# Ordering TensorE's instructions in the mixers' loop of a streaming encoder step: the scheduler's order against the program's order

## The chip, the cores and the metric

The kernel runs on one core of one Trainium2 chip. The metric is the device time of one execution in microseconds (us). Of the kernel before there are three timed runs, whose median is 2215.13 us, and one profiled execution.

## The reference

One layer of a chunk-causal streaming encoder is computed for a prompt of 1024 frames and for a sample of 32 frames that comes with caches, at model width 1024. Three sub-layers follow one another:

```
h = adaln_in(x, ...);  x = x + 0.5 * g1 * rmsnorm(swiglu(h, w1_gate, w1_up, w1_down))
h = adaln_in(x, ...);  q, k, v of both mixers = split(h @ w_in)
oa, ob = mixers(...)
x = x + g2 * rmsnorm(concat([rmsnorm(oa), rmsnorm(ob)]) @ w_out)
h = adaln_in(x, ...);  x = x + 0.5 * g3 * rmsnorm(swiglu(h, w2_gate, w2_up, w2_down))
```

Mixer A is attention with 8 heads of 64, over a frame's own chunk of 64 and the 8 chunks before it. Mixer B has 8 query heads and 2 key and value heads over a window of 128, with a learned sink for each head. Both add a bias by relative distance. The shifts, scales and gates come from a matmul of SiLU(c) with `w_mod`. The newest rows of keys and values are outputs too. Everything is in float32.

## The kernel before, in words

Frames stand in three blocks `TB` of 384, 384 and 288 (the last holds 256 of the prompt and the 32 of the sample). The big products are written as three matmuls in a rounded float32 format: high times high, high times low, low times high (`mm3`, L325 to L327). The kernel goes through a first feed-forward part, the projections and mixers, the output projection, and a second feed-forward part.

The kernel is traced as a program, and a scheduler then puts each engine's instructions in an order of its own: `TileContext(nc, schedule_with_timeline_sim=True)` (L1352) takes, on a modelled clock, of the instructions whose inputs are there, the one that stands earliest in the program. `tc.manual_schedule(engines=...)` around a piece of the program makes the named engines keep the program's order there. The kernel uses that for SP, the engine that issues the transfers, during the start (L119 to L121, closed at L636).

The part around the change is the loop over the mixers' tiles, L1233 to L1269. There are 72 tiles, numbered by `n`. Tiles 0 to 35 are mixer B's: for each of four pairs of heads, one tile of the sample (`TileS`) and eight `TileB` of 128 frames each. Then come mixer A's: 36 to 44 for pair 0, 45 to 53 for pair 1, and from 54 on pairs 2 and 3 in turn, with their sample tiles at 54 and 55. A `TileA` has two halves, one for each head, and its row length L grows from 128 to 640 over the first five of its eight tiles.

A tile has three steps on TensorE, with a softmax between:

- `qk`: scores into PSUM (`S` L752, `Sb` L813 and L814, `Ss` L876 and L877, bank pool `p2` with 2 buffers); then bias add (DVE L754), maximum (DVE L758), exponential (ACT L761), reciprocal and scaling into `P` (L762 to L766).
- `tr`: transposes of `P` into `pp` (L776), `ppb` (L842) or `pps` (L902), in pool `p1` with 3 buffers, copied out to `PT`.
- `av`: `PT` times the values into `po` (L713), pool `pc` with 1 buffer, copied out to `O`. The two heads' matmuls alternate.

In the program, one turn of the loop holds, for each of its two halves: the scores of a tile ahead (two ahead for B, one ahead for A; `scores`, L1224), the transposes of this tile's half, in the first half also the `av` of the tile before, one step of a side task (`step(1)`), one step of the preparation of a coming pair of heads (`prep_step`), and then `fill(rate)`. `fill` puts in pieces of the projections that later tiles need (`pq` of `qk_proj`, `pv` of `v_proj`), so many that they last from turn 0 to 33 and from 37 to 53 (`STAGES`). `prepare` (L1007) loads the cached keys `ck`, writes out the new keys (`pkr`) and transposes the cached ones (`pkc` L1027). From turn 55 on the side tasks are `group_norm` (L1138): two squares on ACT (`sq` L364), sums on POOL (L368, L370), a sum over partitions on TensorE (`pss` L357), a reciprocal root on DVE, then, `WAIT` = 3 steps later, its broadcast on TensorE (`pr` L405), and the scaled values in a high and a low part (`o_hi`, `o_lo`, L1150 to L1155). From turn 67 to 71 each turn begins with one piece of the output projection (`out_piece` L1164, `wo`, 24 matmuls of `mm3`), which first demands that the group norms of its block are done.

Of the kernel before, what the change touches and what calls it, by code (L numbers as in the profile page):

```python
# [60 lines left out]
KB = 0  # L61
SPLIT = "vav"
LEAD_B = 2
MANUAL = False
WAIT = 3
PREP = 3
STAGES = ((0, 34), (37, 54))
# [7 lines left out]
def encoder_step(ctx: ExitStack, tc, x_prompt, x_sample, cache_a_k, cache_a_v, cache_b_k, cache_b_v,  # L75
# [1156 lines left out]

    with tc.manual_schedule(engines={mybir.EngineType.PE}) if MANUAL else ExitStack():  # L1233
        waits[0] = WAIT
# [121 lines left out]
```

## Time and profile before

| what | before |
|---|---|
| median of 3 timed runs | 2215.13 us (2212.06 to 2218.25) |
| the profiled execution's own time | 2217.6 us |
| its span in the profile | 2215.8 us |
| mean granted TensorE clock over the span | 0.984 |
| TensorE busy, share of the span | 98% |
| DVE, ACT, POOL busy, share of the span | 56%, 31%, 8% |
| the mixers' loop in the trace | from 916.6 us to 1329 us |

The rows of the profile name a source line, an engine, an operation and `out<-in` by the names in the program. PE is TensorE. A matmul's busy time is the modelled length of one instruction, and matmuls overlap, so what a matmul takes of TensorE in a run of its like is read from the distance between two starts. `PEclk` is the share of full clock that TensorE was granted. A float32 matmul stands as two records.

### The profile page before, as it was taken

How to read it: one execution, taken by the hardware profiler on the slowest of the kernel's cores; microseconds unless marked ns; L12 is line 12 of the kernel's file. 1: busy time of each engine (PE TensorE's matmuls, PEld its weight loads, DVE VectorE, ACT ScalarE, POOL GpSimd, SP SyncE). 2: the span in 40 equal slices, each digit the busy share in tenths (PEclk: the TensorE clock that was granted, in tenths of full speed). 3: DMA queues.
4: the chain of work that ended last, by engine and by line, in shares of the span. 5: the costliest groups of instructions: out<-in, count | busy, mean ns of one | idle time of the engine just before them, and what ended most of it. 6: DMA issues, size and time to landing. Idle time of an engine off the chain costs nothing.

```text
span 2215.8 us, 33976 instructions
## 1 busy us (share of the span) xinstructions
PE 2161.6 (98%) x14012; PEld 2068.6 (93%) x14012; DVE 1239.1 (56%) x2425; ACT 697.8 (31%) x1450; POOL 179.2 (8%) x281
## 2 busy tenths in 40 slices
PE   6999999999999999899999899999999999999998
PEld 4999999999999999799787589999999999999998
DVE  5788667874333497677444865785333333333336
ACT  4411111111121253576444663542111111111133
POOL 1100000000000023001110313220000000000000
PEclk8999999999999999899999899999999999999999
DMA  9253334434122352111112121424211111111122
GB/s 323 93 153 118 111 96 124 143 101 129 39 66 69 101 184 93 38 39 30 50 30 62 46 77 67 134 86 120 66 58 39 57 39 39 58 38 58 39 69 79
DMA packets 200623, 186.03 MB, mean 84 GB/s; under 512 B 7597, under 2 KB 169813, under 8 KB 199317
## 3 DMA queue, kind: packets, MB, share of 16 engines
q1 hardware_dynamic: 200468, 183.87, 27.1%
q8 instruction: 110, 1.80, 0.3%
q14 instruction: 45, 0.36, 0.1%
HBM read 164.12 MB, written 22.86 MB: 84 GB/s over the span
## 4 chain that ended last, share of the span: by engine, by line
PE 90%; DVE 4%; DMA 3%; ACT 1%; issue 1%; POOL 0%; SPq 0%; ACTq 0%; DVEq 0%; POOLq 0%
PE dn L325 7%; PE dn L326 7%; PE dn L327 7%; PE gate L327 7%; PE gate L326 7%; PE up L327 7%; PE up L326 7%; PE gate L325 7%; PE up L325 7%; PE po L713 3%; PE S L752 2%; PE pq L325 2%; PE pq L327 2%; PE pq L326 2%; DMA raw<-in_w_gate_dram 1%; PE pp L776 1%
## 5 line engine op out<-in xcount | busy, mean ns | idle before, releaser
L326 PE MATMUL gate<-h_lo,w 128*128 128x384 f32 (+1 forms) x1056 | 340.2, 322 | 4.0 <-DVE h_lo L446 4.0
L325 PE MATMUL dn<-gg,w 128*128 128x384 f32 (+1 forms) x1056 | 341.4, 325 | 1.1 <-DVE facc L581 1.0
L581 DVE TENSOR_TENSOR facc<-dn,facc 128x768 f32<-128x768 f32 (+1 forms) x240 | 212.9, 889 | 230.2 <-PE dn L327 229.9
L326 PE MATMUL dn<-gg,w 128*128 128x384 f32 (+1 forms) x1056 | 340.6, 323 | 0.6 <-DVE gg L554 0.6
L325 PE MATMUL gate<-h_hi,w 128*128 128x384 f32 (+1 forms) x1056 | 341.0, 323 | 0.0
L327 PE MATMUL gate<-h_hi,w 128*128 128x384 f32 (+1 forms) x1056 | 340.4, 322 | 0.0
L325 PE MATMUL up<-h_hi,w 128*128 128x384 f32 (+1 forms) x1056 | 340.2, 322 | 0.0
L326 PE MATMUL up<-h_lo,w 128*128 128x384 f32 (+1 forms) x1056 | 340.0, 322 | 0.0
L327 PE MATMUL dn<-gg,w 128*128 128x384 f32 (+1 forms) x1056 | 340.0, 322 | 0.0
L327 PE MATMUL up<-h_hi,w 128*128 128x384 f32 (+1 forms) x1056 | 339.9, 322 | 0.0
L304 DVE TENSOR_TENSOR w<-raw,w 128x1024 fp32r<-128x1024 f32 x187 | 231.5, 1246 | 150.5 <-ACT w L303 150.3
L303 ACT ACTIVATE w<-raw 128x1024 fp32r<-128x1024 f32 x187 | 195.7, 1056 | 266.1 <-PE dn L327 103.5
L550 ACT ACTIVATE sl<-gate 128x384 f32<-128x384 f32 (+1 forms) x132 | 60.9, 462 | 563.9 <-PE gate L327 560.9
L551 DVE TENSOR_TENSOR sl<-sl,up 128x384 f32<-128x384 f32 (+1 forms) x132 | 68.5, 519 | 292.1 <-PE up L327 286.1
L326 PEld LDWEIGHTS gate<-h_lo,w 128*128 128x128 f32 x1056 | 198.6, 188 | 4.6 <-DVE h_lo L446 4.6
L325 PEld LDWEIGHTS dn<-gg,w 128*128 128x128 f32 x1056 | 199.2, 189 | 1.6 <-DVE facc L581 1.2
L326 PEld LDWEIGHTS dn<-gg,w 128*128 128x128 f32 x1056 | 199.2, 189 | 1.0 <-DVE gg L554 0.9
L327 PEld LDWEIGHTS dn<-gg,w 128*128 128x128 f32 x1056 | 199.1, 189 | 0.0
L325 PEld LDWEIGHTS gate<-h_hi,w 128*128 128x128 f32 x1056 | 198.7, 188 | 0.1
L327 PEld LDWEIGHTS gate<-h_hi,w 128*128 128x128 f32 x1056 | 198.7, 188 | 0.0
L327 PEld LDWEIGHTS up<-h_hi,w 128*128 128x128 f32 x1056 | 198.7, 188 | 0.0
L325 PEld LDWEIGHTS up<-h_hi,w 128*128 128x128 f32 x1056 | 198.5, 188 | 0.0
(224 smaller groups left out, 3367.4 us busy)
## 6 DMA issues: line engine op xcount, KB each, us to landing
raw<-in_w_mod_dram SPq DMA_DIRECT2D x56, 512.0 KB, 4.0
raw<-in_w_gate_dram SPq DMA_DIRECT2D x54, 512.0 KB, 4.0
raw<-in_w_up_dram SPq DMA_DIRECT2D x54, 512.0 KB, 4.7
raw<-in_w_down_dram SPq DMA_DIRECT2D x54, 512.0 KB, 4.5
raw<-in_w_in_dram SPq DMA_DIRECT2D x18, 512.0 KB, 4.3
wm<-in_w_mod_dram SPq DMA_DIRECT2D x8, 1024.0 KB, 7.4
raw<-in_w_out_dram SPq DMA_DIRECT2D x13, 512.0 KB, 4.5
xr<-xs SPq DMA_DIRECT2D x16, 384.0 KB, 3.5
```

The lines of the kernel that those rows point to most:

```text
L303: ae.activation(w[:, 0], r, AF.Copy)
L304: ve.tensor_sub(w[:, 1], r, w[:, 0])
L325: te.matmul(ps, w[:, 0, k], hi, start=start, stop=False)
L326: te.matmul(ps, w[:, 0, k], lo, start=False, stop=False)
L327: te.matmul(ps, w[:, 1, k], hi, start=False, stop=stop)
L550: ae.activation(sl[:, :w], ps[0][:, :w], AF.Silu)
L551: ve.tensor_tensor(sl[:, :w], sl[:, :w], ps[1][:, :w], op=OP.mult)
L581: ve.tensor_tensor(o, ps[:, :, :w], o, op=OP.add)
L713: te.matmul(po[64 * h:64 * h + 64, :n], vsl(j, h, kn), PT(h, j, kn), start=j == 0, stop=j == nt - 1)
L752: te.matmul(S[:, c:ce], self.T[:, h, :], KQ[:, 0, 128 * k0 + c:128 * k0 + ce], start=True, stop=True)
L776: te.transpose(pp[:, j - j0, :], P[:, 128 * j:128 * j + 128], ident)
```

## The change

One constant is changed:

```diff
-MANUAL = False
+MANUAL = True
```

It is read at one place, L1233. The block that begins there holds the whole loop, to L1269:

```
    with tc.manual_schedule(engines={mybir.EngineType.PE}) if MANUAL else ExitStack():
        waits[0] = WAIT
...
    tiles[N - 1].av()
```

With it, TensorE's instructions inside the loop stand in the order in which the program traces them. The other engines' instructions, and TensorE's before and after the loop, are still put in order by the scheduler. No instruction is added, removed or changed in shape.

## The prediction

> **What bounds the kernel now.** I read the page's busy shares first, then a table of windows over the loop, the waits of TensorE there, and TensorE's timeline where the table leaves something open.
>
> ```profile
> span 2215.8 us, 33976 instructions
> PE 2161.6 (98%) x14012; PEld 2068.6 (93%) x14012; DVE 1239.1 (56%) x2425; ACT 697.8 (31%) x1450; POOL 179.2 (8%) x281
> ```
>
> TensorE is busy in 98% of the span and no other engine in more than 56%: it is the bound. Only its time in the loop can change, and there only by three things: how long it idles, at what clock it runs, and how much it loses between instructions while it counts as busy. The windows (columns: window, its length, then busy us and records of PE, PEld, DVE, ACT and POOL, granted clock, share of DMA, GB/s) show the first two:
>
> ```profile
> 916.00:922.00 6.00, 3.58 (x25) 2.53 (x23) 4.43 (x15) 3.94 (x14) 0.31 (x1) 0.95 0.42 128
> 922.00:1060.00 138.00, 137.48 (x1078) 125.15 (x1077) 103.97 (x374) 95.91 (x336) 11.14 (x39) 0.99 0.10 28
> 1060.00:1074.00 14.00, 9.80 (x77) 6.93 (x76) 9.26 (x25) 8.79 (x26) 5.28 (x12) 0.91 0.68 190
> 1074.00:1212.00 138.00, 137.86 (x924) 113.68 (x922) 59.95 (x146) 60.20 (x155) 12.26 (x48) 1.00 0.10 26
> 1212.00:1256.00 44.00, 37.66 (x220) 22.92 (x219) 34.13 (x95) 30.12 (x79) 19.14 (x51) 0.81 0.33 93
> 1256.00:1282.00 26.00, 26.00 (x185) 17.91 (x184) 20.93 (x68) 18.20 (x41) 7.06 (x13) 1.00 0.01 1
> 1282.00:1329.00 47.00, 46.34 (x331) 39.17 (x329) 31.42 (x70) 32.34 (x62) 7.61 (x9) 1.00 0.31 90
> ```
>
> In the two long stretches with projections to fill in (922 to 1060, mixer B; 1074 to 1212, mixer A pairs 0 and 1) TensorE idles 0.5 and 0.1 us. It idles 2.4 us at the start, 4.2 us where B passes to A, and 6.3 us from 1212 to 1256, where there is nothing to fill in and the tiles are short; there the clock is 0.81, so that at most 44 x 0.19 = 8.4 us go to a slow clock. From 1256 on it idles 0.7 us. The waits of TensorE from 916 to 1330 name these holes (columns: who waited, for whom, us in all, times, longest):
>
> ```profile
> PE Sb L813 <- ACT Ps L888: 2.4, 1, 2.4
> PE S L752 <- ACT P L761: 2.4, 4, 0.9
> PE po L713 <- ACT o L705: 2.3, 3, 1.3
> ...
> PE pkc L1027 <- DMA ck<-in_cache_a_k_dram: 1.1, 1, 1.1
> ```
>
> **What the order costs where TensorE is busy.** The scheduler's order is near the program's, with one steady difference, seen in one turn of the loop in TensorE's timeline (start, length, what, records merged):
>
> ```profile
> 1116.56 1.24 PE L752 MATMUL S<-KQ,qz 128*128 128x512 f32 x4
> 1117.63 0.71 PE L776 MATMUL pp<-ident,P 128*128 128x128 f32 x5
> 1118.18 1.25 PE L752 MATMUL S<-KQ,qz 128*128 128x512 f32 x4
> 1119.36 0.43 PE L713 MATMUL po<-PT,vt 128*64 128x128 f32 x2
> 1119.72 0.45 PE L325 MATMUL pq<-h_hi,w 128*128 128x384 f32 x1
> 1120.00 0.34 PE L326 MATMUL pq<-h_lo,w 128*128 128x384 f32 x1
> 1120.18 0.33 PE L327 MATMUL pq<-h_hi,w 128*128 128x384 f32 x1
> 1120.35 0.33 PE L325 MATMUL pq<-h_hi,w 128*128 128x384 f32 x1
> ```
>
> A tile's 20 `po` records (L = 640) are not one run: two come as soon as the first head's `PT` is there, the other 18 after the second head's transposes. In the program `av` of a tile stands a turn later, when both are long there, and is one run. What a run costs beside its records comes from the chain of waits, where runs of several lengths stand (start, length, records):
>
> ```profile
> 1104.29 0.80 PE po L713 x10
> 1122.97 1.24 PE po L713 x18
> ```
>
> Eight records more take 0.44 us, so one takes 0.055 and a run has 0.80 - 10 x 0.055 = 0.25 us on top: the lower bound of what one run less saves. The timeline gives the upper one. From the scores at 1118.18 to the third `pq` at 1120.18 are 2.00 us. In them stand the four score records (1.07, as from 1116.56 to 1117.63), two `po` (0.11) and two `pq` (0.35, at 0.17 apiece from the last two rows): 1.53 us. So 0.47 us are lost around this run. I take 0.40, nearer to the timeline's, because there the neighbours' delay is counted too.
>
> How many runs go: I counted along TensorE's timeline. From 1074 to 1212 there are 35 runs of `po` for 16 tiles (the first and the last below; 13 + 3 copies of `po` to `o` count the tiles), so 19 go. From 1256 to 1329 there are 23 for 11 tiles, so 12 go. In the B stretch there are 36 for 36, and nothing goes. From 1212 to 1256 three go in a stretch with holes, which I count at nothing.
>
> ```profile
> 1077.29 0.66 PE L713 MATMUL po<-PTs,aux 128*64 128x32 f32 x16
> ...
> L705 ACT ACTIVATE o<-po x13: 197/277/287, 1078.2 to 1207.9; 128x128 f32<-128x128 f32 x11, 128x32 f32<-128x32 f32 x2
> L703 DVE COPY o<-po x3: 291/292/293, 1105.1 to 1171.1; 128x128 f32<-128x128 f32 x3
> ...
> 1210.88 1.31 PE L713 MATMUL po<-PT,vt 128*64 128x128 f32 x18
> ```
>
> Both stretches are TensorE's (137.86 of 138, 26.00 of 26, 46.34 of 47 us), so the saving is on the path: 31 x 0.40 = **12.4 us** (7.8 to 14.6).
>
> **What stands in its way.** In the program's order a step that waits holds up all TensorE work behind it. Where there is fill, I find the cover enough. For L = 640 a softmax takes, by the groups of DVE and ACT from 1212 to 1330 (columns: group, count, busy us, mean ns):
>
> ```profile
> L758 DVE TENSOR_REDUCE nm<-S 128x1 f32<-128x640 f32 x16 | 13.1, 819 | 0.2
> L754 DVE TENSOR_TENSOR S<-S,aux 128x256 f32<-128x256 f32 x28 | 12.0, 430 | 8.8 <-PE S L752 8.3
> L761 ACT ACTIVATE P<-S,nm 128x640 f32<-128x640 f32 x17 | 13.4, 790 | 3.9 <-DVE nm L758 3.0 <-DVE den L762 0.9
> L764 ACT ACTIVATE P<-P,den 128x640 f32<-128x640 f32 x7 | 5.8, 826 | 1.6 <-DVE den L762 1.5
> ```
>
> That is 0.43 + 0.82 + 0.79 + 0.83 = 2.9 us, with the small steps and the hand-overs an estimated 4. Between a half's scores and its transposes the program puts one turn: of this tile two scores (2.14), two rounds of transposes (5 at 0.11 each, from 1117.63 to 1118.18: 1.1) and `po` (1.24), 4.5 us, and with fill more. So with fill nothing waits; without it the cover is 0.5 us. For short tiles it is less, which is why the hole from 1212 to 1256 stays as it is in my sum: the two buffers of `p2` set it, whatever the order.
>
> New waits, each bounded from both sides:
> - Start: the transposes of tile 0 now stand ahead of the scores of tile 3, which today cover part of the softmax: four matmuls of 256 columns, 4 x 0.17 x 256/384 = 0.45 us, or 0.9 at half clock. 0.6 us (0 to 0.9).
> - B to A, 1060 to 1074: `pkc` waits for the cached keys, with the last tiles of B and the first scores of A behind it on TensorE, and DVE behind those. One `po` run of B, which today runs before that wait, now comes after it: 0.25 + 8 x 0.055 = 0.7 us (from -1.1, the wait gone, to +2.8, the whole landing of the transfer of `ck`, next row).
>
> ```profile
> DMA to landing us min/median/max: 2.8/2.8/2.8
> ```
>
> - Group norms: `pss` stands one half turn, some 2.2 us, behind the second square. Before it come that square and two sums on POOL:
>
> ```profile
> L364 ACT ACTIVATE sq<-o x12: 667/838/846, 1222.9 to 1343.1; 128x768 f32<-128x768 f32 x8, 128x576 f32<-128x576 f32 x4
> L368 POOL TENSOR_TENSOR sq<-sq x11: 797/998/1267, 1223.9 to 1330.7; 128x384 f32<-128x384 f32 x8, 128x288 f32<-128x288 f32 x3
> L370 POOL TENSOR_TENSOR sq<-sq x5: 791/994/2002, 1225.9 to 1332.0; 128x384 f32<-128x384 f32 x4, 128x288 f32<-128x288 f32 x1
> ```
>
>   0.84 + 1.0 + 1.0 = 2.8 us, so 0.6 us each, four times in the loop: 2.4 us (0, if ACT and POOL take the squares early, to 4 x 2.8 = 11.2). Behind a waiting `pss` stand the next half's scores and this half's transposes, and DVE and ACT wait for those. `pr` has three half turns, 6.6 us, for a dozen short steps on DVE: nothing.
> - The first `out_piece`, at the head of turn 67: `o_lo` of its block comes from a square-root chain that is forced just before, and that turn's scores, transposes and `po` stand behind it. 2.0 us (0 to 4, two sums of this kind):
>
> ```profile
> L1155 POOL TENSOR_TENSOR o_lo<-z,o_hi x6: 1749/1858/2469, 1239.2 to 1358.7; 128x768 fp32r<-128x768 f32 x4, 128x576 fp32r<-128x576 f32 x2
> ```
>
> The change moves no transfer. SP, DVE, ACT and POOL get a new order from the scheduler, which I cost at nothing because none of them is busy for more than 81% of any window above (DVE from 1256 to 1282). Together the new waits are 0.6 + 0.7 + 2.4 + 2.0 = 5.7 us. Net gain 12.4 - 5.7 = 6.7 us against the profiled execution's 2217.6 us: 2210.9. That execution lies 2.5 us above the median of 2215.13, so on the median's scale the forecast is **2208.4 us**, 0.3% less. 0.3%, or 6.6 us, is about what a measurement of this kernel can tell from no change.
>
> **Does a wait cost more than its length?** After the 2.38 us of idling at the start, matmuls of the same shape start 0.32 us apart at first, against 0.17 later:
>
> ```profile
> 920.53 0.39 PE L813 MATMUL Sb<-KSB,qs 128*128 128x256 f32 x1 [2.38 <-ACT Ps L888]
> 924.09 0.52 PE L326 MATMUL pq<-h_lo,w 128*128 128x384 f32 x1
> 924.41 0.52 PE L327 MATMUL pq<-h_hi,w 128*128 128x384 f32 x1
> 924.94 0.34 PE L326 MATMUL pq<-h_lo,w 128*128 128x384 f32 x1
> ```
>
> They are slow from about 921 to 924.7: 3.5 us at half speed, 1.7 us lost on top of a wait of 2.4. I let waits of 2 us and less cost themselves alone, and charge 1.7 us for each longer one. The Trainium skill, "TensorE: Matmul & The Clock Gate", Part 1, states that the clock falls to half only after an idle window of about 3.4 us. By that rule waits of 2.8 us would cost no clock, and the slow rival below would be 6.8 us cheaper; the row of 2.38 us speaks against it here, since the fall came after a shorter wait.
>
> **The rivals.**
> - *The new waits decide* (slower). Each `pss` finds nothing done early and TensorE stands still for the whole chain: 4 x 2.8 = 11.2 us, 4 x 1.7 = 6.8 for the clock, 4 at the first `out_piece`, 0.9 + 2.8 at the start and at B to A, together 25.7 against 12.4 saved: 2215.1 + 13.3 = 2228.4 us. For it: POOL's second sum took up to 2.0 us (its longest above). Against it: ACT, which starts the chain, is free for some 30% of these stretches (18.20 of 26, 32.34 of 47 us busy). It turns slower by 0.3% once the new waits together pass 12.4 + 6.6 = 19 us.
> - *The hole closes too* (faster). With `po` out of the way the score steps follow one another sooner from 1212 to 1256, and the slow clock there goes by half with the idle time: (6.3 + 8.4) / 2 = 7.3 us more: 2201.1 us. Against it: DVE is busy 34.13 of 44 us there, and its order is still the scheduler's.
> - *Nothing to gain.* The 0.40 us beside a `po` run are no loss of TensorE's but hide in the softmaxes: DVE and ACT become late as soon as TensorE is quicker, most of all from 1256 to 1282 (DVE 20.93 of 26 us). 2215 us. That the order does not change at all is a case of this; the count of 35 runs for 16 tiles speaks against it.
>
> **How the numbers follow.** Forecast 0.50, about half of it beyond 0.3% on the fast side, and I lean to faster: 0.30 faster, 0.20 same; its own range is 2203 to 2213 from the bounds of the saving. Slow rival 0.22. Hole closes 0.18. Nothing to gain 0.10. Faster 0.30 + 0.18 = 0.48, same 0.20 + 0.10 = 0.30, slower 0.22. The range reaches from 2197 (the hole and the upper bound of the saving) to 2226, which leaves out the far half of the slow rival.
>
> **What would show it.** In the changed profile: 16 runs of `po` for 16 tiles in the stretch of A with fill, and that stretch 7 to 8 us shorter; B's stretch of 138 us the same within 2; `pss` rows with idle time for POOL `sq`, under 1 us each; the first `wo` with a wait for `o_hi` or `o_lo` of some 2 us; the stretch of short tiles still near 44 us with a clock near 0.8. Waits of TensorE for P or PT in a stretch with fill would prove the cover wrong; `pss` waits of 2 us and more, or a clock under 0.95 after 1256, mean the slow rival.

## The result and the profile after

The changed kernel takes **2234.61 us** (2231.30 to 2235.27) against 2215.30 us of before (2212.06 to 2218.25): a ratio of 1.0084, 95% interval 1.0067 to 1.0102. It is slower by 0.8%; 2208.4 us was forecast, and the range ended at 2226. Its profiled execution took 2235.27 us, with a span of 2233.3 us and a mean clock of 0.979. One execution of seg_short (11936 us) and two of after_short (2374 and 3512 us), runs described further down, took far longer than the others of their kernels and are left out of the medians below.

To find the time, I cut the loop of both kernels at the same seven points: the first score, the last `Sb` of B, the first `pq` of A, the last `pq`, the first `wo`, the last `po`, and the first matmul of the second feed-forward part. These are the windows of before and then of after (window, length, then busy us and records of PE, PEld, DVE, ACT and POOL, granted clock, DMA share, GB/s):

```profile
917.00:1060.00 143.00, 140.06 (x1095) 127.25 (x1094) 107.59 (x387) 99.45 (x349) 11.45 (x40) 0.99 0.11 31
1060.00:1073.00 13.00, 8.80 (x74) 5.93 (x73) 8.26 (x21) 8.67 (x25) 5.20 (x12) 0.95 0.65 181
1073.00:1203.00 130.00, 129.86 (x856) 108.45 (x855) 55.49 (x138) 55.84 (x141) 10.51 (x41) 0.99 0.10 26
1203.00:1282.00 79.00, 72.66 (x474) 47.06 (x473) 60.53 (x174) 52.80 (x133) 28.03 (x72) 0.89 0.21 58
1282.00:1329.00 47.00, 46.34 (x331) 39.17 (x329) 31.42 (x70) 32.34 (x62) 7.61 (x9) 1.00 0.31 90
1329.00:1414.00 85.00, 81.83 (x522) 80.64 (x522) 55.88 (x113) 35.92 (x60) 29.43 (x20) 0.96 0.26 88
```

```profile
916.00:1066.00 150.00, 142.79 (x1096) 128.44 (x1096) 108.83 (x387) 100.84 (x349) 11.84 (x40) 0.98 0.11 30
1066.00:1085.00 19.00, 13.10 (x93) 8.38 (x91) 9.65 (x25) 9.26 (x27) 2.75 (x12) 0.67 0.51 141
1085.00:1210.00 125.00, 124.24 (x840) 107.31 (x839) 55.92 (x136) 56.46 (x142) 9.79 (x40) 0.98 0.09 25
1210.00:1292.00 82.00, 66.23 (x462) 44.77 (x460) 56.36 (x164) 50.53 (x127) 24.84 (x68) 0.85 0.20 56
1292.00:1349.00 57.00, 51.94 (x352) 44.62 (x350) 34.56 (x78) 33.86 (x65) 10.59 (x14) 0.94 0.25 75
1349.00:1435.00 86.00, 81.17 (x517) 80.20 (x516) 55.86 (x113) 36.24 (x61) 29.41 (x20) 0.96 0.27 89
```

Three numbers come out of each row: *idle* is the length less PE's busy time; *clock* is what the slow clock cost, PE's busy time times (1 - granted clock); *rest* is what is left, TensorE's work at full clock. Summed over the six rows:

| us | loop | idle | clock | rest |
|---|---|---|---|---|
| before | 497 | 17.4 | 14.4 | 465.1 |
| after | 519 | 39.5 | 26.0 | 453.5 |
| difference | +22.0 | +22.1 | +11.6 | -11.6 |

So the saving is there and nearly as large as forecast (12.4), but the new waits cost 33.7 us where 5.7 had been charged. (The clock has two decimals, so a sum of *clock* is good to some 2 us. The span grew by 17.5 us and not by 22: the windows are cut at whole microseconds, the loop began 0.7 us earlier, and the second feed-forward part happened to be 2.9 us shorter in this execution.) By stage, idle time grew by 4.3 us in B, 1.7 in the passage from B to A, 0.6 in A with fill, 9.4 among the short tiles, 4.4 around the output pieces and 1.7 behind them. A with fill is the one stage that got shorter, by 5 us.

TensorE's waits from 916 to 1350 us in after, the largest first, to set beside the largest of before in the prediction (who waited, for whom, us in all, times, longest). Of before's other waits in the loop none was longer than 1.5 us.

```profile
PE pkc L1027 <- DMA ck<-in_cache_a_k_dram: 4.6, 2, 3.2
PE ppb L842 <- ACT Pb L830: 4.4, 5, 1.5
PE pp L776 <- ACT P L764: 3.8, 3, 3.0
PE pps L902 <- DVE Ps L892: 3.4, 2, 2.0
PE S L752 <- ACT P L761: 2.6, 2, 1.5
PE po L713 <- ACT o L705: 2.3, 1, 2.3
PE wo L326 <- DVE o_lo L1155: 1.9, 1, 1.9
PE wo L326 <- POOL o_lo L1155: 1.7, 1, 1.7
PE Sb L813 <- ACT Ps L888: 1.7, 1, 1.7
PE pss L357 <- POOL sq L370: 1.4, 2, 1.2
PE wo L325 <- ACT o_hi L1154: 1.1, 1, 1.1
```

No single wait is the loss. There are many of 1 to 3 us, in all stages but one, and more than half of the time in these rows is for a softmax (`Pb`, `P`, `Ps`).

**How one of them comes about in B.** The transposes of a full tile start at 969.43 us, after 1.49 us of waiting; its scores had started at 960.25. First TensorE, then DVE between the two, then one line of ACT (start, length, what):

```profile
960.25 0.28 PE L813 MATMUL Sb<-KSB,qs 128*128 128x256 f32 x1
...
967.67 0.28 PE L814 MATMUL Sb<-KSB,qs 128*128 128x256 f32 x1
969.43 0.66 PE L842 MATMUL ppb<-ident,Pb 128*128 128x128 f32 x4 [1.49 <-ACT Pb L830]
```

```profile
960.92 0.70 DVE L815 TENSOR_TENSOR Sb<-Sb,bias 128x512 f32<-128x512 f32 x1 [1.20 <-PE Sb L814]
...
962.22 0.69 DVE L817 TENSOR_REDUCE nmb<-Sb 128x2 f32<-128x512 f32 x1
962.95 0.28 DVE L724 TENSOR_TENSOR qs<-qbt,qs 64x128 fp32r<-64x128 f32 x1
963.15 1.21 DVE L320 TENSOR_TENSOR w<-raw,w 128x1024 fp32r<-128x1024 f32 x1
...
964.72 0.16 DVE L818 TENSOR_TENSOR nmb<-nmb,nsk 128x2 f32<-128x2 f32 x1
...
966.29 0.69 DVE L817 TENSOR_REDUCE nmb<-Sb 128x2 f32<-128x512 f32 x1
967.01 0.60 DVE L724 TENSOR_TENSOR qs<-qbt,qs 64x128 fp32r<-64x128 f32 x2
...
967.78 0.16 DVE L826 TENSOR_TENSOR denb<-denb,es 128x2 f32<-128x2 f32 x1
...
968.30 0.16 DVE L827 RECIPROCAL denb<-denb 128x2 f32<-128x2 f32 x1
```

```profile
966.69 0.20 ACT L825 ACTIVATE es<-es 128x2 f32<-128x2 f32 x1
```

From the first score at 960.25 until its transposes stand at the head of TensorE's queue at 967.94 (969.43 less the wait), this tile has two turns of the program: 7.7 us. Its softmax took 9.2, counted from the same first score. Its own steps are short, but the small ones stand in DVE's queue: the maximum is done at 962.91, and the 0.16 us step on it starts 1.8 us later, behind the splitting of a weight (1.21 us). The sum at 967.78 has its last input from ACT at 966.89 and starts 0.9 us later, behind the splitting of queries. In before no `ppb` waits anywhere in B: there TensorE has taken other work until the softmax was done.

**The passage and the first output piece.** SP issues the load of `ck` at 1068.73 us, behind the store of `kr`, and `pkc` reaches the head of TensorE's queue when the load is still on its way. (In before the load stands behind the same store, at 1062.41 us, and `pkc` waits 1.1 us for it instead of 3.21.) At 1291.92 TensorE begins the first output piece, whose `o_hi` and `o_lo` are not there:

```profile
1068.24 0.38 SPq L998 DMA_DIRECT2D out_dram<-kr  x1
1068.73 0.44 SPq L1021 DMA_DIRECT2D ck<-in_cache_a_k_dram  x1
```

```profile
1071.87 0.63 PE L1027 MATMUL pkc<-ident,ck 128*128 128x128 f32 x4 [3.21 <-DMA ck<-in_cache_a_k_dram]
...
1080.04 0.69 PE L902 MATMUL pps<-ident,Ps 64*128 64x64 f32 x4 [2.00 <-DVE Ps L892]
...
1294.04 0.44 PE L326 MATMUL wo<-o_lo,w 128*128 128x384 f32 x1 [1.70 <-POOL o_lo L1155]
...
1296.23 0.45 PE L325 MATMUL wo<-o_hi,w 128*128 128x384 f32 x1 [1.05 <-ACT o_hi L1154]
1298.54 0.69 PE L326 MATMUL wo<-o_lo,w 128*128 128x384 f32 x1 [1.86 <-DVE o_lo L1155]
1299.03 0.52 PE L327 MATMUL wo<-o_hi,w 128*128 128x384 f32 x1
1299.35 0.52 PE L325 MATMUL wo<-o_hi,w 128*128 128x384 f32 x1
```

The waits call the slow clock: from 1299.03 on matmuls start 0.32 us apart instead of 0.17, and the passage runs at a mean clock of 0.67. The piece lasts from 1291.92 to 1304.14, 12.2 us for 24 matmuls that take 24 x 0.17 = 4.1 us at full clock.

### The profile page after: what moved, and what is told of

Its sections match the earlier page's. It is cut to its first block, busy times and chain, and to the rows that moved or that the text cites. A ratio compares the mean times of both kernels' runs of the same rounds, so it can differ in the third digit from the quotient of the medians.

```text
span 2233.3 us, 33966 instructions
## 1 busy us (share of the span) xinstructions
PE 2156.6 (97%) x14012; PEld 2068.7 (93%) x14012; DVE 1240.6 (56%) x2425; ACT 699.2 (31%) x1450; POOL 176.6 (8%) x281
## 4 chain that ended last, share of the span: by engine, by line
PE 87%; DVE 6%; DMA 4%; ACT 2%; issue 1%; POOL 0%; SPq 0%; ACTq 0%; DVEq 0%; POOLq 0%
PE dn L325 7%; PE dn L326 7%; PE gate L327 7%; PE dn L327 7%; PE gate L326 7%; PE gate L325 7%; PE up L326 7%; PE up L325 7%; PE up L327 7%; PE pq L325 2%; PE S L752 2%; PE pq L326 2%; PE pq L327 2%; PE po L713 2%; PE wo L325 1%; PE wo L326 1%
## 5 line engine op out<-in xcount | busy, mean ns | idle before, releaser
L327 PEld LDWEIGHTS up<-h_hi,w 128*128 128x128 f32 x1056 | 198.4, 188 | 0.0
L326 PEld LDWEIGHTS up<-h_lo,w 128*128 128x128 f32 x1056 | 198.3, 188 | 0.0
```

The lines of the kernel that those rows point to most:

```text
L326: te.matmul(ps, w[:, 0, k], lo, start=False, stop=False)
L327: te.matmul(ps, w[:, 1, k], hi, start=False, stop=stop)
```

## The experiments

The expectations speak of four theories. *H*: the loss is the sum of waits at the head of TensorE's queue at a few places. *G*: it is the new order of the other engines. *R*: a run of `po` costs 0.25 to 0.47 us beside its records. *C*, formed later: in the program's order the work between a tile's scores and its transposes is shorter than its softmax, wherever that happens. The last columns are cut and worked out as above; they come from one execution of each kernel, which can lie some us from the median (seg_short's took 2216.40 us, against a median of 2220.47). Ratios are to the kernel before, measured beside each. All kernels have the same 832 records of `po`.

| kernel | median us | ratio (95%) | runs of `po` | loop | idle | clock | rest |
|---|---|---|---|---|---|---|---|
| before | | | 106 | 497 | 17.4 | 14.4 | 465.1 |
| after | 2234.61 | 1.0084 (1.0067-1.0102) | 73 | 519 | 39.5 | 26.0 | 453.5 |
| seg_b | 2228.51 | 1.0057 (1.0045-1.0069) | 103 | 509 | 24.9 | 17.1 | 466.9 |
| seg_a | 2214.71 | 0.9997 (0.9988-1.0006) | 84 | 491 | 22.3 | 10.0 | 458.7 |
| seg_short | 2220.47 | 1.0021 (1.0012-1.0029) | 93 | 499 | 24.2 | 12.9 | 461.8 |
| seg_out | 2219.85 | 1.0020 (1.0011-1.0030) | 100 | 500 | 22.4 | 14.9 | 462.8 |
| head1_first | 2208.45 | 0.9955 (0.9942-0.9969) | 81 | 490 | 21.3 | 13.8 | 454.9 |
| after_split | 2241.61 | 1.0110 (1.0097-1.0123) | 102 | 522 | 33.4 | 22.5 | 466.1 |
| after_ck | 2234.09 | 1.0074 (1.0062-1.0086) | 73 | 512 | 38.0 | 23.5 | 450.5 |
| after_out68 | 2230.73 | 1.0067 (1.0054-1.0080) | 73 | 516 | 36.8 | 22.6 | 456.5 |
| after_trb | 2237.12 | 1.0097 (1.0083-1.0110) | 73 | 515 | 40.1 | 23.0 | 451.9 |
| after_lead36 | 2234.07 | 1.0081 (1.0066-1.0096) | 73 | 512 | 34.0 | 24.7 | 453.4 |
| after_all | 2226.66 | 1.0048 (1.0033-1.0063) | 73 | 511 | 39.0 | 20.1 | 451.9 |
| best_a | 2218.49 | 1.0009 (0.9999-1.0019) | 75 | 494 | 26.7 | 13.2 | 454.1 |
| before_short | 2214.19 | 0.9990 (0.9982-0.9999) | 106 | 494 | 15.0 | 14.8 | 464.2 |
| after_short | 2219.31 | 1.0014 (1.0005-1.0024) | 73 | 498 | 28.2 | 18.6 | 451.1 |
| after_pda | 2358.74 | 1.0639 (1.0625-1.0653) | 73 | 641 | 122.1 | 56.2 | 462.7 |
| head1_ck | 2214.42 | 0.9990 (0.9981-0.9998) | 83 | 494 | 22.0 | 17.7 | 454.3 |

### The change in one stretch of the loop at a time

The program's order holds for the turns from a first to a last one only (here 37 to 53, seg_a):

```diff
-    with tc.manual_schedule(engines={mybir.EngineType.PE}) if MANUAL else ExitStack():
+    pe_order = ExitStack()
+    with pe_order:
...
         for n in range(N):
+            if n == 37:
+                pe_order.enter_context(tc.manual_schedule(engines={mybir.EngineType.PE}))
+            if n == 54:
+                pe_order.close()
```

seg_b, turns 0 to 36:

> The program's order for turns 0 to 36 alone (mixer B and the passage to A), the scheduler's elsewhere. Theory H (heads of the queue): the change's loss sits where a waiting step holds up all TensorE work behind it; in the two traces this part is 9.9 us later at the first projection piece of A (12.5 us later at 1085.0 against 1072.5, minus what is recovered), so 13 us slower than before, +8 to +15. Theory G (global): the loss comes from the new order of DVE, ACT, POOL and SP over the whole loop and cannot be cut by stretches; then a stretch alone shows another sum, here within 3 us of before. The prediction on record had +1.3 us for this part.

seg_a, turns 37 to 53:

> The program's order for turns 37 to 53 alone (mixer A, pairs 0 and 1, with projections to fill in). Theory H: this stretch has no new waits and 19 runs of po fewer; the two traces show it 6.4 us shorter, so 6 to 8 us faster than before (0.3%), which would beat both kernels. Theory G: within 3 us of before, since the other engines' order elsewhere is the scheduler's old one. The prediction on record had 7.6 us faster for this part.

seg_short, turns 54 to 66:

> The program's order for turns 54 to 66 alone (short tiles of pairs 2 and 3, no projections, group norms beside). Theory H: 4 us slower (the two traces: from the first Ss of this part to the first wo 69.6 us before, 73.8 after), +2 to +7, with pss waiting for POOL. Theory G: within 3 us of before. The prediction on record had +2.4 us less what it counted at nothing.

seg_out, turns 67 to 71:

> The program's order for turns 67 to 71 alone (an output-projection piece at the head of each turn). Theory H: the first piece stands still for o_hi and o_lo with the turn behind it; 10 us slower (47.1 us from the first wo to the last po before, 57.3 after), +5 to +11. Theory G: within 3 us of before. The prediction on record had 2.0 us of waiting less 4.8 us saved by 12 runs of po fewer, so 2.8 us faster.

The medians moved by +12.3, -1.5, +4.2 and +3.6 us against the kernel before beside them. The sum is +18.6, and the whole change gave 2234.61 - 2215.30 = +19.3: the parts add up, within the 2 us or so to which each is known. The largest is B with the passage, which I had charged with nothing but 0.6 at its start and 0.7 at its end. seg_b and seg_short came out as theory H expected. seg_a and seg_out did not: seg_a gave 1.5 us instead of 6 to 8, which is no difference that the runs can tell from none, and seg_out cost 3.6 instead of 5 to 11. The sum speaks against theory G; seg_a taken alone would not. In seg_a's trace the stretch with fill takes 123 us instead of 130, as expected; but the short tiles, which stand in the scheduler's order there as before, took 83 us instead of 79 (11.3 us idle instead of 6.3). The traced execution, at 2210.06 us its fastest, still has a loop 6 us shorter than before's; the median of 2214.71 shows 1.5. Where the slower executions lost their time stands in no trace and is left open.

### The price of a run of `po`, without the program's order

head1_first is the kernel before, with the two heads' matmuls exchanged, so that the first `po` needs the later head's `PT` and the scheduler cannot start a tile's `po` early. after_split is the changed kernel with A's `po` cut in two, the first matmul in its old place and the rest half a turn later.

```diff
-            for h in range(2):
+            for h in (1, 0):
                 te.matmul(po[64 * h:64 * h + 64, :n], vsl(j, h, kn), PT(h, j, kn), start=j == 0, stop=j == nt - 1)
```

```diff
+        part(todo_mm[:1])
+        if two:
+            cut.append(rest)
...
                     tiles[n - 1].av()
+                if half == 1 and cut:
+                    cut.pop()()
```

> The kernel before (scheduler's order everywhere), only the two heads' matmuls of po written with the second head first, so that po can't begin before the second head's PT is there: 81 runs of po instead of 106 on TensorE, and no other change. Theory R (a run of po costs 0.25 to 0.47 us of TensorE beside its records): 25 x 0.40 = 10 us faster than before (6 to 12), about 2206. Rival (the run's cost lies beside waits of the softmaxes, or is given back later, as the loss of seg_a's gain hints): within 3 us of before.

> The changed kernel, with po of each of mixer A's 32 tiles cut in two as the scheduler cut it: one matmul in the first half of a turn, the rest in the second; 102 runs instead of 73. Theory R: 29 x 0.40 = 11.6 us slower than the changed kernel (7 to 14), so 1.0135 of before. Rival: no more than 3 us slower than the changed kernel, 1.0084 of before.

head1_first has 25 runs less and is 9.1 us faster than before (2208.45 against 2217.56). after_split has 29 runs more than after and is 5.8 us by the difference of the ratios (1.0110 - 1.0084) slower, half of what was expected and between the ranges of theory R (7 to 14) and its rival (no more than 3); its *rest* grew by 12.6, and 6.1 us less of idle time and 3.5 less of clock gave most of it back. By *rest* a run costs (465.1 - 453.5) / 33 = 0.35 us between before and after, 12.6 / 29 = 0.43 us between after_split and after, and 10.2 / 25 = 0.41 us between before and head1_first. So theory R holds for TensorE's work; how much of it reaches the kernel's time depends on the waits beside it. The Trainium skill, "TensorEngine Tiling", section "Tiling Modes", says that a change of the tiling mode drains TensorE. The records of `po` (128*64) stand between records of 128*128, so these 0.35 to 0.43 us are what that page would lead one to look for; it gives no figure, and no run here shows what the time goes into.

### Single repairs of the changed kernel

after_ck loads `ck` two turns earlier; after_out68 holds the output pieces back by a turn; after_trb does all of a B tile's transposes in the second half of its turn; after_lead36 is after_ck with tile 36 scored two turns ahead like B's tiles; after_all has all four. (Tile 36 is the first of mixer A's, a sample tile, and not B's last, as the expectation has it.)

```diff
+            for key in opens.get(n + PREP + 2, []):
+                if key[0] == "A":
+                    prep["ck", key[1]] = load_ck(key[1])
```

```diff
-OUTS = (0,) * 13 + (1,) * 5
+OUTS = (0,) * 14 + (1,) * 4
```

```diff
-            if hh:
+            if not hh:
                 return
             nt = self.nt
```

```diff
-        return LEAD_B if t < 36 else 1
+        return LEAD_B if t < 37 else 1
```

> The changed kernel, with the load of the cached keys ck traced two turns earlier, so that it stands ahead of the store of kr on SP's queue. Theory H: the 3.2 us of pkc waiting at 1071.9 (and 1.4 at 1217.6) go, with part of the 17.1 us at half clock behind it: 5 to 9 us faster than the changed kernel, about 1.005 of before. Rival: the softmaxes of the sample tile and the first A tile are the next thing late there (2.0 us of pps waiting behind), so that only 0 to 3 us are won, 1.007 to 1.0084 of before.

> The changed kernel, with the first output-projection piece at turn 68 instead of 67 and the fifth after the loop, so that two more half turns lie between the group norm and the first wo. Theory H: of the waits of wo for o_hi and o_lo (1.7 + 1.1 + 1.9 = 4.7 us in the changed kernel) at least 3.5 us go, and some 3 us of half clock behind them: 5 to 8 us faster than the changed kernel, about 1.0055 of before. Rival: those tiles are as slow without the piece, since their softmaxes are not covered by it: 0 to 2 us, 1.0075 to 1.0084 of before.

> The kernel after, with B's transposes of the softmax (the second stage of a sample turn) all done in the second half of the turn instead of half by half, so that the softmax of the first half has half a turn more before TensorE asks for it. Theory H (the 6.7 us that the sample stage grew by are waits of `ppb` for ScalarE's L830 at the head of TensorE's queue): those waits, 4.4 us in 5 from 916 to 1350 us in the changed kernel, go for the most part, and the time falls by 4 to 6 us against the changed kernel, to about 1.006 of before. Rival (VectorE and ScalarE are simply behind in this order, whatever TensorE asks first): the waits move to another tile and the time falls by 0 to 2 us.

> The kernel after_ck (ck loaded two turns earlier) with the scores of sample tile 36, the last of B's, led by as many turns as its other tiles. In after_ck the wait at the passage had moved from `pkc` (DMA) to `pps`, which waited 4.61 us in one for VectorE's Ps. Theory H (waits in the passage add up with the half clock that they call): that wait goes and with it part of the some 10 us at half clock behind it, 5 to 9 us less than after_ck, about 1.004 of before. Rival (the passage is a chain that only moves from one wait to the next): 0 to 2 us less.

> A test of closure: the kernel after with all four repairs together: ck loaded earlier (it gave 2.2 us), the scores of sample tile 36 led like the others, B's transposes of the softmax in the second half of a turn, and the output pieces kept off the first four late turns (it gave 3.8 us). If theory H is complete (the loss is the sum of waits at the head of TensorE's queue in these places): after less 2.2, less 5 to 9, less 4 to 6, less 3.8, so about 2215 to 2219, 0.999 to 1.002 of before. If the loss lies in something else that comes with the order: 2225 or above, 1.004 or more.

Each repaired its wait, and little came of it: by the ratios after_ck won 2.2 us and after_out68 3.8, both within what the intervals leave open, and after_trb and after_lead36 won nothing. In after_ck `pkc` no longer waits in the passage, but `pps` behind it waits 4.61 us for DVE instead of 2.00. after_lead36 removes that too (0.8 us are left, and the passage is 14 us instead of 17 and 19), but the loop is 512 us long as in after_ck: the short tiles take 81 us instead of 79, at a clock of 0.81 instead of 0.85, and the stage behind them is longer too. In after_trb the waits for `Pb` are gone from B, and this stands in their place (waits, from 918 to 1070 us):

```profile
PE po L713 <- ACT PTb L705: 7.3, 14, 1.7
```

after_all was expected at 2215 to 2219 and took 2226.66 us. By the ratios that is 8 us less than after, more than the four repairs gave singly, and 11 us are still missing. Its *idle* is 39.0 us, hardly less than after's 39.5; most of the gain is in the clock (20.1 against 26.0). As a list of four places, theory H fails: in these traces, when one wait is taken away, the next step behind it waits instead.

### The length of the softmax, and the order of the other engines

before_short and after_short take the row maximum over 64 of a row's columns in the tiles of A and B. The reference's maximum over the whole row is left out, and nothing else is changed:

```diff
-            ve.tensor_reduce(nm, S[:, :L], axis=AX.X, op=OP.max, negate=True)
+            ve.tensor_reduce(nm, S[:, L - 128:L - 64], axis=AX.X, op=OP.max, negate=True)
...
-            ve.tensor_reduce(nm, S[:, :, :L], axis=AX.X, op=OP.max, negate=True)
+            ve.tensor_reduce(nm, S[:, :, L - 128:L - 64], axis=AX.X, op=OP.max, negate=True)
```

after_pda puts VectorE and ScalarE in the program's order as well:

```diff
-    with tc.manual_schedule(engines={mybir.EngineType.PE}) if MANUAL else ExitStack():
+    with tc.manual_schedule(engines={mybir.EngineType.PE, mybir.EngineType.DVE, mybir.EngineType.Activation}) if MANUAL else ExitStack():
```

> The kernel before with the maximum of a row taken over 64 of its columns in place of all 128 to 640 (tiles of A and B; the reference's maximum over the whole row is left out, the reduction of 819 ns becomes one of some 150 to 200 ns). Theory C (in the program's order TensorE waits because the softmax is longer than the work that the program puts between scores and transposes): the scheduler's order already puts other work there, so only its hole at the short tiles shrinks, 0 to 6 us faster than before. Rival (DVE's load sets the pace in both orders): as much faster as after_short is against after, over 6 us.

> The changed kernel with the same shorter maximum. Theory C: TensorE's idle time in the loop falls from 39.5 us by 10 us or more, the half clock with it, and the time falls by 10 to 20 us against the changed kernel, at least 8 us more than before_short does against before. Rival (the waits come from the new order of the other engines, or from transfers and POOL): it falls by no more than before_short's gain and 3 us.

> The changed kernel with VectorE's and ScalarE's instructions in the program's order inside the loop too. Theory G (the loss comes from the order that the scheduler gives the other engines once TensorE's is fixed): 5 us or more faster than the changed kernel. Theory C (it is the length of the softmax against its cover): no gain; VectorE and ScalarE now wait at the heads of their own queues as well, 0 to 40 us slower than the changed kernel.

The same shorter step is worth 2.0 us in the scheduler's order (2214.19 against 2216.20) and 15.3 us in the program's (2219.31 against 2234.61). Idle time falls by 2.4 us in the one and by 11.3 in the other, and the cost of the clock by 7.4 in the other. Here are B's stage and the short tiles of after_short, and its waits in B (918 to 1060 us), to be held against 150 and 82 us and against `ppb`'s 4.4 in 5 above:

```profile
916.00:1060.00 144.00, 140.90 (x1091) 128.01 (x1092) 98.19 (x386) 100.68 (x348) 11.56 (x40) 0.98 0.11 33
1199.00:1277.00 78.00, 64.73 (x459) 44.39 (x458) 47.08 (x162) 50.14 (x127) 24.96 (x67) 0.87 0.21 59
```

```profile
PE Sb L813 <- ACT Ps L888: 1.7, 1, 1.7
PE ppb L842 <- ACT Pb L830: 0.7, 1, 0.7
```

B is back to a microsecond from before's 143 us, though TensorE still stands in the program's order there. That is theory C: the length of the softmax against its cover. Its rival, a load of DVE that sets the pace in both orders, would have sped up both kernels alike. The shorter step shortens the chain and empties DVE's queue at once, and the runs don't tell these two apart. Not all is explained by it: 28.2 us idle remain against 15.0, for the transfer of `ck`, the group norms, the output pieces and the rest of the softmax.

The two traces also say whether the softmaxes themselves became longer, as theory G would have it. I took, for each tile of B and each half of a tile of A, the time from its first score to the end of its scaling, and the time from its first score to its first transpose (us):

| | softmax before: mean (longest) | softmax after | to the transposes before: mean | after |
|---|---|---|---|---|
| B, 32 tiles | 7.4 (9.5) | 6.8 (9.1) | 10.0 | 9.4 |
| A with fill (pairs 0 and 1), 32 halves | 4.7 (9.5) | 4.2 (6.2) | 10.5 | 9.1 |
| A's short tiles (L up to 512, pairs 2 and 3), 16 halves | 5.6 (8.8) | 5.0 (7.2) | 8.8 | 6.4 |

The softmaxes did not become longer. What the change took away is the time until TensorE asks for their result, most of all at the short tiles. On the mean that time is still enough; it is for the longer softmaxes that TensorE waits, and those the scheduler's order let be late.

after_pda refutes theory G in the form that I gave it: with the other engines in the program's order too the kernel is 124 us slower than after, three times the most that I had expected. It does not give the other engines the order that they had in before; no run does, and for that the table above has to stand. after_pda's largest waits, from 915 to 1112 us, are scores that wait for the queries' high parts, at work on ACT:

```profile
PE Sb L813 <- ACT qs L721: 25.9, 17, 3.4
```

### A better kernel than both

best_a is seg_a with head1_first's order of the heads; head1_ck is head1_first with `ck` loaded earlier.

> The program's order in turns 37 to 53 only (where seg_a gave 0 to 1.5 us) together with the order of the heads of head1_first (which gave 10 us): 75 runs of `po` in place of 106 and of head1_first's 81. If a run costs 0.35 to 0.40 us and nothing else changes: 2 to 2.5 us below head1_first, about 0.9945 of before. If the program's order in A has a cost of its own that ate up the saving in seg_a: no better than head1_first, 0.9955 or above.

> head1_first (10 us faster than before, with the scheduler's order) with ck loaded two turns earlier. Its waits for that transfer are 3.6 us in 2: if they go, 2 to 3.6 us below head1_first, 0.994 to 0.9945 of before. If another wait comes in their place, as in after_ck: 0.995 to 0.9965.

Neither beats head1_first, which stays the fastest, 9.1 us below before; best_a, expected 2 us below it, is no faster than before, and head1_ck hardly. All three have nearly the same *rest* (454.9, 454.1, 454.3); they differ in *idle* and *clock* together: 35.1, 39.9 and 39.7 us. Most of the difference lies behind the last `pq`, where each has the scheduler's own order, and each a different one. So changes earlier in the loop went with differences of some 5 us behind the last `pq`, where they change nothing themselves. Why one of these orders is the better I have not settled.

## Why the prediction was wrong, point by point

- **The saving, 12.4 us (31 runs by 0.40).** Right, with some luck: 33 runs went, two more than counted, and *rest* fell by 11.6 us, so 0.35 a run instead of 0.40; the two errors offset each other. The stretch with fill was forecast 7 to 8 us shorter and is 5: its *rest* fell by 6.8 us (128.6 to 121.8), and 1.8 came back as waits and clock.
- **"So with fill nothing waits."** This step failed, and with the passage it cost most. I had compared cover and softmax once, for a tile of A with L = 640, and there it held (0.6 us more idle time). For B I made no such comparison and forecast its 138 us "the same within 2". In B the softmax shares DVE with the splitting of weights and queries, takes 9.2 us in the tile shown and has 7.7. B's stage is 150 us instead of 143, and seg_b, which holds the passage too, is 12.3 us slower than before.
- **The sum of single steps as the length of a softmax.** 2.9 us of steps, "an estimated 4", counted each step's duration and not its place in the queue of its engine. To conclude from busy shares (none above 81% of a window) that the other engines cost nothing was the same mistake: DVE is 73% busy in B (108.83 of 150 us), and a step of 0.16 us still stood 1.8 us in its queue. It was not their *new* order that cost it; B's softmaxes took 7.4 us on the mean in before already, and there the scheduler covered them.
- **The short tiles, whose hole "stays as it is in my sum".** Failed. Idle time there went from 6.3 to 15.8 us; *rest* fell by 8.4 us (64.7 to 56.3), in part for the saved runs and in part because work fell on the other side of the cut. seg_short alone is 4.2 us slower. I had put the hole down to "the two buffers of `p2`", "whatever the order"; with the same two buffers the order alone took the time until the transposes from 8.8 us to 6.4. That I had computed the cover there as less than 0.5 us myself should have warned me.
- **B to A, 0.7 us (-1.1 to +2.8).** The wait for `ck` grew from 1.1 to 3.21 us, by 2.1: three times the term, but inside its range. What was missing is what follows: 2.00 us for `Ps`, and the clock. The passage grew from 13 to 19 us. A second wait for `ck`, 1.4 us among the short tiles, was not in the sum either.
- **Group norms, 2.4 us (0 to 11.2).** Inside the range, but little more than half the size: `pss` waits 1.4 us in 2 inside the loop, against none in before. `pr`, put at nothing, waits 1.3 us in 2 for DVE.
- **The first output piece, 2.0 us (0 to 4).** Right in kind, too small: 1.70 + 1.05 + 1.86 = 4.6 us of waits, and half clock for what was left of the piece, 12.2 us instead of 4.1 in all. after_out68 won 3.8 us back (1.0084 - 1.0067 of 2216), within what the intervals leave open.
- **The clock.** "Waits of 2 us and less cost themselves alone" failed where several stood close together: it gave no clock at all to the forecast's waits, and *clock* grew by 11.6 us. For B's waits, of up to 1.5 us and apart from each other, it held (last section).
- **The rivals.** "The new waits decide" was the right one, chance 0.22, at 2228.4 us, 6 us too low. Its threshold (19 us of new waits) was passed. Its places were half wrong: it put 11.2 us on the group norms and nothing on B and the short tiles. Two of the promised signs stand in the trace: waits for P in a stretch with fill (`Pb`, in B), and a clock of 0.94 at the output pieces. "The hole closes too" is refuted by the row of the short tiles.

## What to carry to other kernels

When an engine is put into a fixed order, compare for every kind of tile, in every stage, the time between two of its steps with the whole chain of the other engines in between, queueing included, and not for the one tile whose softmax looks longest. Waits on the bounding engine can cost more than themselves: over this loop about half as much again by the clock (22.1 us idle, 11.6 us clock), nothing where they were short and apart, and more where they came together. And where the gain hangs on one property of an order, here that a tile's `po` records are one run, get that property by itself: two heads exchanged gave 9 us where the whole order lost 19.

## What the runs showed of the hardware

TensorE's clock fell after shorter waits than I had allowed for, where they stood close together. Here are the start of the loop, the rest of B, and the first output piece in after, cut where the granted clock changes (columns as before; the clock is the third number from the end), and the wait at the start:

```profile
915.60:919.00 3.40, 1.78 (x15) 1.04 (x14) 2.74 (x8) 2.37 (x6) 0.00 (x0) 1.00 0.39 83
919.00:925.80 6.80, 6.09 (x20) 5.67 (x21) 4.45 (x20) 4.09 (x18) 0.31 (x1) 0.50 0.17 58
926.00:1066.00 140.00, 135.12 (x1065) 121.72 (x1063) 102.04 (x360) 94.17 (x326) 11.53 (x39) 1.00 0.10 28
1294.47:1297.88 3.41, 1.16 (x6) 0.57 (x4) 3.39 (x9) 1.47 (x2) 1.22 (x5) 1.00 0.00 0
1297.88:1304.70 6.82, 6.16 (x18) 5.94 (x19) 1.23 (x3) 0.57 (x3) 0.00 (x0) 0.50 0.01 2
```

```profile
919.71 0.58 PE L813 MATMUL Sb<-KSB,qs 128*128 128x256 f32 x1 [1.70 <-ACT Ps L888]
```

At the start the clock is half from 919.0 us on, 0.7 us before the wait of 1.70 us is over; a wait of 0.63 us stands just ahead of it, and in the 3.4 us before the fall TensorE was busy for 1.78. At the first output piece, with its waits of 1.70, 1.05 and 1.86 us, it was busy for 1.16 of the 3.41 us before the fall. In B from 926 us on, where the waits are no longer than 1.5 us and stand apart, the clock is 1.00 throughout, with 4.9 us idle in all. The Trainium skill, "TensorE: Matmul & The Clock Gate", Part 1, asks for an idle window of about 3.4 us; the traces here disagree, since TensorE was partly busy in the 3.4 us before each of these two falls.
